# Rotary embedding on one core: tile 2 loaded whole ahead of the first store, tile 3 loaded in halves behind it, and the first store tied to a subtraction of tile 1

## The chip, the cores and the metric

The kernel runs on one core of a Trainium2 chip. The metric is the device time of one execution in microseconds, taken as the median of several executions; less is better. Beside the times there is a profile of one execution, whose time axis starts at its first instruction.

## The reference, cut to what matters

`x` has the shape (16, 512, 16, 64) in float32: batch, position, heads, 64 elements. `cos` and `sin` have the shape (512, 32), of which only the first 16 columns are used. Of each row of 64 elements the first 32 are rotated in two quarters of 16, and the last 32 pass through:

```python
rotated_first  = x1[..., :16] * cos[..., :16] - x1[..., 16:] * sin[..., :16]
rotated_second = x1[..., :16] * sin[..., :16] + x1[..., 16:] * cos[..., :16]
out = concatenate([rotated_first, rotated_second, x2], axis=-1)
```

So 33.55 MB come in and 33.55 MB go out, and each of the rotated elements costs two multiplications and one addition or subtraction.

## The kernel before, in words

The array is cut into four tiles (`T` = 4), each of 128 partitions by 16 positions (`K` = 16, called rows here) of 1,024 elements: 64 KB in each partition, 8.39 MB in a tile. A ring in SBUF holds three tiles (`NS` = 3), so that tile 3 lies where tile 0 lay, and can only be loaded when tile 0 has been stored. All loads and the stores of tiles 0, 1 and 3 are issued by SP (`load` L56, `store` L59) on one queue; the store of tile 2 and the two small loads of the tables are issued by POOL on another. SP issues in the order of the program, and an instruction that waits holds up all that is behind it on SP.

VectorE (DVE) does all the arithmetic. It first spreads the tables (L62 to L84). Then `rotate(t, lo, hi)` works rows `lo` to `hi` of tile `t` in four instructions: the product with the sine into the PSUM buffer `b_t` (L97), the product with the cosine in place (L98), a subtraction into the first quarter (L99), and an addition into the second (L106). Most calls take 8 rows, half a tile (`KC` = 8); tile 2 is worked in 8, 5 and 3 rows (`KM` = 5).

The order of the transfers is written out by hand. SP issues: load of tile 0, load of tile 1, load of the second half of tile 2; store of the first half of tile 0, store of its second half; load of the first half of tile 2, load of tile 3; store of tile 1; store of tile 3. The function `hold` ties a transfer to an instruction of DVE that it doesn't need for its data, so that it is issued no earlier than that. It is used twice: the first store of tile 0 waits for the first part of the last addition of tile 0, which is cut at row 12 for this (`KP`), and the store of tile 1 waits for the subtraction of the 5 rows of tile 2 (`near`).

Of the kernel before, what the change touches and what calls it, by code (L numbers as in the profile page):

```python
# [1 line left out]

# [4 lines left out]


@with_exitstack
def kernel(  # L10
    ctx: ExitStack,
    tc: tile.TileContext,
    x: bass.AP,
    cos: bass.AP,
    sin: bass.AP,
    out: bass.AP,
):
    nc = tc.nc
    fp32 = mybir.dt.float32
    P = 128  # L20
    B, S, H, D = x.shape
    Q = D // 4
    HF = D // 2

    K = 16
    T = B * S // (P * K)
    PB = S // K
    REP = P // PB  # L30
    R = H * D
    NS = 3
    KC = K // 2
    KM = 5
    KP = K - 4

    xf = x.rearrange("b s h d -> (b s h d)").rearrange("(t p f) -> t p f", t=T, p=P)
    of = out.rearrange("b s h d -> (b s h d)").rearrange("(t p f) -> t p f", t=T, p=P)
    cosf = cos.rearrange("(p k) j -> p (k j)", k=K)
    sinf = sin.rearrange("(p k) j -> p (k j)", k=K)  # L40

    const_pool = ctx.enter_context(tc.tile_pool(name="const", bufs=1))
    b_pool = ctx.enter_context(tc.tile_pool(name="bp", bufs=1, space=bass.MemoryType.PSUM))


    ring = const_pool.tile([P, NS, K, H, D], fp32)
    stage = const_pool.tile([P, 2, K, HF], fp32)
    spun = const_pool.tile([P, 2 * K, Q], fp32)
    packed = const_pool.tile([PB, 2 * K, Q], fp32)
    table = const_pool.tile([P, 2, K, 2, Q], fp32)  # L50

    def rows(t, lo, hi):
        return ring[:, t % NS, lo:hi].rearrange("p k h d -> p (k h d)")

    def load(t, lo=0, hi=K):
        return nc.sync.dma_start(out=rows(t, lo, hi), in_=xf[t, :, lo * R : hi * R])  # L56

    def store(t, lo=0, hi=K, queue=nc.sync):
        return queue.dma_start(out=of[t, :, lo * R : hi * R], in_=rows(t, lo, hi))  # L59


    nc.vector.memset(stage[:, :, :, 0:Q], 0.0)  # L62
    spread = stage.rearrange("(j b) t k i -> j b t (k i)", b=REP)
    nc.gpsimd.dma_start(out=spread[:, 0, 0], in_=cosf)  # L64
    nc.gpsimd.dma_start(out=spread[:, 0, 1], in_=sinf)  # L65
    load(0)
    load(1)
    load(2, KC, K)

    PQ = PB // REP
    nc.vector.stream_shuffle(  # L74
        out=spun[:],
        in_=stage.rearrange("p t k j -> p (t k) j")[:, :, 0:Q],
        mask=[j % PQ * REP for j in range(PB)],
    )
    for q in reversed(range(REP)):
        n = PQ * (q + 1)  # L80
        nc.vector.tensor_copy(out=packed[0:n], in_=spun[q * PB : q * PB + n])  # L81

    for r in range(REP):
        nc.vector.tensor_copy(  # L84
            out=table[r * PB : (r + 1) * PB].rearrange("p t k c j -> p (t k) c j"),
            in_=packed.unsqueeze(2).to_broadcast((PB, 2 * K, 2, Q)),
        )
    C = table[:, 0].rearrange("p k c j -> p k (c j)")
    Sn = table[:, 1].rearrange("p k c j -> p k (c j)")

    def rotate(t, lo, hi, cut=None):
        x1 = ring[:, t % NS, lo:hi, :, 0:HF]
        c = C[:, lo:hi].unsqueeze(2).to_broadcast((P, hi - lo, H, HF))
        s = Sn[:, lo:hi].unsqueeze(2).to_broadcast((P, hi - lo, H, HF))
        b_full = b_pool.tile([P, KC, H, HF], fp32, name="b_t")
        b_t = b_full[:, 0 : hi - lo]
        nc.vector.tensor_mul(out=b_t, in0=x1, in1=s)  # L97
        nc.vector.tensor_mul(out=x1, in0=x1, in1=c)  # L98
        first = nc.vector.tensor_sub(  # L99
            out=x1[:, :, :, 0:Q], in0=x1[:, :, :, 0:Q], in1=b_t[:, :, :, Q:HF]  # L100
        )
        ends = [hi - lo] if cut is None else [cut - lo, hi - lo]
        done = []
        for a, b in zip([0] + ends, ends):
            done.append(
                nc.vector.tensor_add(  # L106
                    out=x1[:, a:b, :, Q:HF],
                    in0=x1[:, a:b, :, Q:HF],
                    in1=b_t[:, a:b, :, 0:Q],
                )  # L110
            )
        return first, done

    def hold(transfer, point):
        tc.add_manual_dep(
            transfer.ins,
            point.ins.name,
            mybir.DependencyInfo(
                mybir.DependencyClass.Sync, mybir.DependencyReason.DATA
            ),  # L120
            reason="the store follows the loads at the DMA engines",
        )

    rotate(0, 0, KC)
    _, close = rotate(0, KC, K, cut=KP)
    hold(store(0, 0, KC), close[0])
    store(0, KC, K)
    load(2, 0, KC)
    load(3)
    rotate(1, 0, KC)  # L130
    rotate(1, KC, K)
    behind_loads = store(1)
    rotate(2, KC, K)
    near, _ = rotate(2, 0, KM)
    rotate(2, KM, KC)
    store(2, queue=nc.gpsimd)

    hold(behind_loads, near)
    rotate(3, 0, KC)
    rotate(3, KC, K)  # L140
    store(3)


# [1 line left out]
_INS = ['x', 'cos', 'sin']  # L145
_OUTS = [((16, 512, 16, 64), 'float32')]


# [23 lines left out]
```

## Time and profile before

| What | Value |
| --- | --- |
| Median of 3 runs | 161.93 us (161.56 to 161.94) |
| The profiled execution's own time | 161.67 us |
| Its span, first to last instruction | 159.8 us |
| DVE busy | 113.0 us (71%), 48 instructions |
| POOL busy | 1.9 us (1%) |
| Moved by DMA | 67.24 MB in 1504 packets |
| Load of tile 0, issue to landing | 22.2 us |
| Store of tile 1 (L59), issued at | 97.59 us |
| Store of tile 3 (L59), issued at | 131.32 us |

A span of 159.8 us lies inside a time of 161.67 us: 1.87 us are outside the first and last instruction. DMA share is the mean busy share of the 16 DMA engines; since a packet is counted where it starts and lasts up to 2.4 us, a short window can show more than 1.00, and windows that begin and end at packet borders are the ones to trust. "Issue to landing" is the time from the instruction on the queue to the arrival of the last byte; with several transfers queued it holds the wait for those ahead.

### The profile page before, as it was taken

What the parts mean: (1) busy time and instruction counts of PE and PEld (TensorE: products, weight loads), DVE (VectorE), ACT (ScalarE), POOL (GpSimd) and SP (SyncE); (2) the same over time, 40 slices, a digit from 0 to 9 for tenths busy, and PEclk for the clock granted to TensorE, in tenths of its full rate; (3) what the DMA queues carried; (4) which work ended last, traced back from release to release, by engine and by line L of the source; (5) the groups of instructions that cost most, each with busy time, mean ns of one, the idle gap of its engine ahead of it and who ended that gap; (6) DMA issues with size and microseconds to landing.
All of it is one profiled execution on the core that took longest, in us unless ns stands there. A gap on an engine that the chain in (4) does not pass through costs nothing.

```text
span 159.8 us, 120 instructions
## 1 busy us (share of the span) xinstructions
DVE 113.0 (71%) x48; POOL 1.9 (1%) x7
## 2 busy tenths in 40 slices
DVE  1000959999999999999999999999999980000000
POOL 3000000000000000000000000010000000000000
DMA  7969989899799999999999799996996996996990
GB/s 262 541 262 541 410 377 525 377 410 525 303 467 410 394 484 426 402 402 508 402 525 476 312 525 394 394 525 295 492 525 262 525 508 279 525 508 279 525 508 16
DMA packets 1504, 67.24 MB, mean 421 GB/s; under 512 B 192, under 2 KB 192, under 8 KB 224
## 3 DMA queue, kind: packets, MB, share of 16 engines
q1 hardware_dynamic: 1296, 58.72, 85.4%
q0 software_dynamic: 208, 8.52, 12.3%
HBM read 33.69 MB, written 33.55 MB: 421 GB/s over the span
## 4 chain that ended last, share of the span: by engine, by line
DVE 61%; DMA 14%; issue 5%; DVEq 1%
DVE b_t L97 22%; DVE ring L98 22%; DMA ring<-in_x_dram 14%; DVE ring L106 10%; DVE ring L99 7%; DVEq L167 1%; DVEq L97 0%
## 5 line engine op out<-in xcount | busy, mean ns | idle before, releaser
L97 DVE TENSOR_TENSOR b_t<-ring,table 128x4096 f32<-128x4096 f32 (+2 forms) x9 | 35.6, 3958 | 2.1 <-DMA ring<-in_x_dram 1.9
L98 DVE TENSOR_TENSOR ring<-ring,table 128x4096 f32<-128x4096 f32 (+2 forms) x9 | 35.6, 3950 | 0.3
L99 DVE TENSOR_TENSOR ring<-ring,b_t 128x2048 f32<-128x2048 f32 (+2 forms) x9 | 18.4, 2050 | 0.3
L106 DVE TENSOR_TENSOR ring<-ring,b_t 128x2048 f32<-128x2048 f32 (+3 forms) x10 | 18.4, 1853 | 0.0
L74 DVE LOAD_MASK_SELECT spun<-stage x1 | 0.0, 14 | 14.4 <-DMA stage<-in_sin_dram 14.4
L84 DVE COPY table<-packed 32x1024 f32<-32x1024 f32 x4 | 2.7, 684 | 0.1
L59 POOL DMA_DIRECT2D out_dram<-ring x1 | 0.6, 562 | 101.8 <-DVE ring L106 101.8
L81 DVE COPY packed<-spun 32x512 f32<-32x512 f32 (+3 forms) x4 | 1.7, 416 | 0.1
L62 DVE MEMSET stage<- 128x512 f32 x1 | 0.5, 485 | 0.9 <-PEq L156 0.9
L74 DVE STREAM_SHUFFLE spun<-stage 128x512 f32<-128x512 f32 x1 | 0.7, 721 | 0.0
L64 POOL DMA_DIRECT2D stage<-in_cos_dram x1 | 0.6, 644 | 1.3 <-DVE stage L62 1.3
L65 POOL DMA_DIRECT2D stage<-in_sin_dram x1 | 0.5, 535 | 0.0
L156 POOL MEMSET const-bfloat16-1.0<- 128x1 bf16 x1 | 0.1, 102 | 0.0
L156 POOL MEMSET const-float32-0.0<- 128x1 f32 x1 | 0.1, 99 | 0.2 <-issue 0.2
L156 POOL MEMSET const-float32-1.0<- 128x1 f32 x1 | 0.1, 99 | 0.0
L156 POOL MEMSET const-uint8-127<- 128x1 uint8 x1 | 0.1, 99 | 0.0
## 6 DMA issues: line engine op xcount, KB each, us to landing
ring<-in_x_dram SPq DMA_DIRECT2D x2, 4096.0 KB, 40.8
out_dram<-ring SPq DMA_DIRECT2D x2, 4096.0 KB, 17.4
stage<-in_cos_dram POOLq DMA_DIRECT2D x1, 64.0 KB, 9.0
stage<-in_sin_dram POOLq DMA_DIRECT2D x1, 64.0 KB, 13.4
ring<-in_x_dram SPq DMA_DIRECT2D x3, 28.9
out_dram<-ring SPq DMA_DIRECT2D x2, 31.1
out_dram<-ring POOLq DMA_DIRECT2D x1, 39.6
```

The lines of the kernel that those rows point to most:

```text
L59: return queue.dma_start(out=of[t, :, lo * R : hi * R], in_=rows(t, lo, hi))
L62: nc.vector.memset(stage[:, :, :, 0:Q], 0.0)
L64: nc.gpsimd.dma_start(out=spread[:, 0, 0], in_=cosf)
L65: nc.gpsimd.dma_start(out=spread[:, 0, 1], in_=sinf)
L74: nc.vector.stream_shuffle(out=spun[:], in_=stage.rearrange("p t k j -> p (t k) j")[:, :, 0:Q], mask=[j % PQ * REP for j in range(PB)],)
L81: nc.vector.tensor_copy(out=packed[0:n], in_=spun[q * PB : q * PB + n])
L84: nc.vector.tensor_copy(out=table[r * PB : (r + 1) * PB].rearrange("p t k c j -> p (t k) c j"), in_=packed.unsqueeze(2).to_broadcast((PB, ...
L97: nc.vector.tensor_mul(out=b_t, in0=x1, in1=s)
L98: nc.vector.tensor_mul(out=x1, in0=x1, in1=c)
L99: first = nc.vector.tensor_sub(out=x1[:, :, :, 0:Q], in0=x1[:, :, :, 0:Q], in1=b_t[:, :, :, Q:HF])
L106: nc.vector.tensor_add(out=x1[:, a:b, :, Q:HF], in0=x1[:, a:b, :, Q:HF], in1=b_t[:, a:b, :, 0:Q],)
L167: with _tile.TileContext(nc) as tc:
```

## The change

Tile 2 is loaded whole as the third load. Tile 3 is loaded in two halves, one issued behind the landing of each half of the store of tile 0. The two stores of tile 0 are written behind both rotations of tile 0, and the first of them is held by the subtraction of the first 5 rows of tile 1. Tile 1 is worked in 5, 5 and 6 rows where it was worked in 8 and 8. The cut addition of tile 0 becomes one instruction again. Tile 2 is worked in 8, 5 and 3 rows as before, but from its first row on. The store of tile 1 is tied to another instruction of the 5 rows there: to the product with the cosine (L97 after, L98 before), and no longer to the subtraction (L98 after, L99 before) that follows it.

```diff
     load(0)
     load(1)
-    load(2, KC, K)
+    load(2)
...
     rotate(0, 0, KC)
-    _, close = rotate(0, KC, K, cut=KP)
-    hold(store(0, 0, KC), close[0])
-    store(0, KC, K)
-    load(2, 0, KC)
-    load(3)
-    rotate(1, 0, KC)
-    rotate(1, KC, K)
+    rotate(0, KC, K)
+    halves = [(0, KC), (KC, K)]
+    behind_loads = [store(0, lo, hi) for lo, hi in halves][0]
+    for lo, hi in halves:
+        load(3, lo, hi)
+    _, near = rotate(1, 0, KM)
+    hold(behind_loads, near)
+    rotate(1, KM, 2 * KM)
+    rotate(1, 2 * KM, K)
     behind_loads = store(1)
-    rotate(2, KC, K)
-    near, _ = rotate(2, 0, KM)
-    rotate(2, KM, KC)
+    rotate(2, 0, KC)
+    near, _ = rotate(2, KC, KC + KM)
+    hold(behind_loads, near)
+    rotate(2, KC + KM, K)
     store(2, queue=nc.gpsimd)
 
-    hold(behind_loads, near)
     rotate(3, 0, KC)
     rotate(3, KC, K)
     store(3)
```

`rotate` loses its argument `cut` and returns two other instructions: the product with the cosine (`scaled`) and the subtraction (`first`). So `near` stands for two things. For tile 1 it is the second value returned, the subtraction; for tile 2 it is the first, the product. The lines of the changed file that say so:

```python
        scaled = nc.vector.tensor_mul(out=x1, in0=x1, in1=c)
...
        return scaled, first
```

More of the change, by code (lines that the diff above doesn't have):

```diff
@@ L34 @@
     KM = 5
-    KP = K - 4
     xf = x.rearrange("b s h d -> (b s h d)").rearrange("(t p f) -> t p f", t=T, p=P)
@@ L89, with rotate @@
     Sn = table[:, 1].rearrange("p k c j -> p k (c j)")
-    def rotate(t, lo, hi, cut=None):
+    def rotate(t, lo, hi):
         x1 = ring[:, t % NS, lo:hi, :, 0:HF]
@@ L97, in rotate @@
         nc.vector.tensor_mul(out=b_t, in0=x1, in1=s)
-        nc.vector.tensor_mul(out=x1, in0=x1, in1=c)
+        scaled = nc.vector.tensor_mul(out=x1, in0=x1, in1=c)
         first = nc.vector.tensor_sub(
@@ L101, in rotate @@
         )
[L102 to L112, printed above, removed]
+        nc.vector.tensor_add(
+            out=x1[:, :, :, Q:HF], in0=x1[:, :, :, Q:HF], in1=b_t[:, :, :, 0:Q]
+        )
+        return scaled, first
     def hold(transfer, point):
```

## The prediction

> **What bounds the kernel now.** I read the page's DMA parts first, then the chain of work that ended last, then the busy time by window cut at the stages, and last the timeline around the instructions that release stores.
>
> ```profile
> DVE 61%; DMA 14%; issue 5%; DVEq 1%
> ...
> q1 hardware_dynamic: 1296, 58.72, 85.4%
> q0 software_dynamic: 208, 8.52, 12.3%
> HBM read 33.69 MB, written 33.55 MB: 421 GB/s over the span
> ```
>
> The chain names DVE for 61% of the span, and on that alone the kernel looks bound by arithmetic. The two queues speak against it: their packets fill 85.4 + 12.3 = 97.7% of all 16 DMA engines' span. The chain follows semaphores, and a store that was released by DVE but then stands behind other bytes is told as DVE's. So the question is whether DMA ever stood still. The windows, cut at the borders of the stages (columns: window, length, DVE busy, POOL busy, clock, DMA share, GB/s):
>
> ```profile
> 1.70:51.00 49.30, 32.86 (x20) 1.18 (x2) 1.00 1.00 428
> 51.10:70.60 19.50, 19.36 (x6) 0.00 (x0) 1.00 1.00 430
> 70.60:99.80 29.20, 28.92 (x12) 0.00 (x0) 1.00 1.00 431
> 99.80:158.50 58.70, 31.22 (x12) 0.56 (x1) 1.00 0.99 429
> ```
>
> The first row is loads alone, the second the stores of tile 0 alone, the third loads again, the fourth the last three stores. The share is 0.99 to 1.00 in each, and reading and writing run at the same 428 to 431 GB/s. From 1.70 to 158.50 us the DMA engines do nothing but move the bytes that must be moved. The time is therefore 1.70 us ahead of the first byte, 156.80 us of full DMA, 1.30 us to the end of the span at 159.8, and 1.87 us outside it: 161.67 us. DVE ends its last instruction at 131.3 us and is 27 us early.
>
> The changeover from loads to the store of tile 1 shows no hole either (borders at packet ends; same columns):
>
> ```profile
> 97.39:99.80 2.41, 2.38 (x3) 0.00 (x0) 1.00 1.01 435
> 99.80:102.22 2.42, 2.39 (x2) 0.00 (x0) 1.00 1.00 433
> 102.22:104.64 2.42, 2.35 (x4) 0.00 (x0) 1.00 1.00 433
> ```
>
> **The change part by part.** The bytes are the same. SP still issues nine transfers: four of half tiles and five of whole ones become again four and five (a half load of tile 2 twice and half stores twice, against half stores twice and half loads of tile 3 twice). So DMA's own work is the same 156.80 us, and the change costs or saves only where it opens or closes a hole. I therefore time DVE first, and then lay each issue of SP against what is still queued.
>
> The rows that price DVE (start, duration, engine, line, operation; the row of SPq merges the issues of the last two stores on SP, and starts with that of tile 1):
>
> ```profile
> 36.51 4.43 DVE L97 TENSOR_TENSOR b_t<-ring,table 128x4096 f32<-128x4096 f32 x1
> ...
> 50.02 4.43 DVE L97 TENSOR_TENSOR b_t<-ring,table 128x4096 f32<-128x4096 f32 x1
> ...
> 90.35 2.83 DVE L97 TENSOR_TENSOR b_t<-ring,table 128x2560 f32<-128x2560 f32 x1
> 93.22 2.83 DVE L98 TENSOR_TENSOR ring<-ring,table 128x2560 f32<-128x2560 f32 x1
> 96.08 1.49 DVE L99 TENSOR_TENSOR ring<-ring,b_t 128x1280 f32<-128x1280 f32 x1
> ...
> 97.59 34.08 SPq L59 DMA_DIRECT2D out_dram<-ring  x2
> 99.00 1.77 DVE L97 TENSOR_TENSOR b_t<-ring,table 128x1536 f32<-128x1536 f32 x1
> ...
> 104.44 4.43 DVE L97 TENSOR_TENSOR b_t<-ring,table 128x4096 f32<-128x4096 f32 x1
> ```
>
> Five rows take 99.00 - 90.35 = 8.65 us, three take 104.44 - 99.00 = 5.44, eight take 13.44 (36.51 less the 23.07 at which the first call starts). Six lie on the line between five and eight: 8.65 + 4.79 / 3 = 10.25.
>
> The cut addition goes: the second half of tile 0 took 50.02 - 36.51 = 13.51 and takes 13.44, so tile 1 starts at 49.95. Tile 1 in 5, 5 and 6 rows costs 8.65 + 8.65 + 10.25 = 27.55 against 2 x 13.44 = 26.88; tile 2 starts at 77.50, against 76.91 before: **DVE is 0.59 us later from there to its end**, since tiles 2 and 3 keep their sizes. Tile 2's whole load lands at about 61.7 us (below), 16 us ahead of its use, so DVE doesn't wait.
>
> *First store.* It waits for the subtraction of tile 1's first five rows, which ends 97.57 - 90.35 = 7.22 us into such a call: 49.95 + 7.22 = 57.17 us (48.88 before). Behind it on SP stand the second store of tile 0 and both loads of tile 3, the latter needing this store's landing anyway. The loads ahead now end half a tile later: load 1 landed at 42.3 us (issued 1.17, 41.1 to landing) and load 0 at 23.0, so a tile takes 19.3 and load 2 lands at 61.7. The store is queued 4.5 us before that; before the change it was 52.15 - 48.88 = 3.3. No hole; were the cover gone, each us of lateness would be a us of the end.
>
> *Loads of tile 3.* Half a tile takes 9.7 to 9.9 us (the two half stores landed at 61.9 and 71.8). The first half store lands at 61.7 + 9.9 = 71.6, the seventh half tile, as the second half store was before. SP issues the first half load then, with the second half store, 9.7 us of bytes, still running. That lands at about 81.5, and the second half load is issued with the first, again 9.7 us, in front of it. Loads end at about 100.8, as before (71.91 + 28.9). DVE wants these halves at 105.0 and 118.5. Cost: nothing, hidden by the half transfer in front each time.
>
> *Store of tile 1.* Here the diff does more than its words say. In tile 2 `near` is now the first value returned, the product with the cosine, and no longer the subtraction. The product ends 93.22 + 2.83 - 90.35 = 5.70 us into the call: 77.50 + 13.44 + 5.70 = 96.64, so the issue comes at 96.66, 0.93 us earlier than the 97.59 before in spite of DVE's delay. The lead over the end of loads grows from 3.2 to 4.1 us. Cost: nothing, for the profile shows no hole with the shorter lead.
>
> *Stores of tiles 2 and 3.* POOL's store is issued at 104.71 + 0.59 = 105.3, with nearly all of tile 1's 19 us queued in front. SP's last store is issued at 131.32 + 0.59 = 131.91. It took 27.5 us from issue to landing (the list of DMA issues, cut at that instant), against 19.3 for a tile alone: 8.2 us of other bytes were in front, 7.6 stay. Cost: nothing.
>
> *Could there be a price that the trace doesn't show?* Stores are now issued with leads of 4.5 and 4.1 us. Generating their descriptors beside running transfers could slow these; the rows around the first release (49.88:51.09, share 1.03 for 1.21 us) allow 0.04 us each. From below, the most that any order could win is the time in which DMA runs under its best rate: 67.24 MB at 433 GB/s is 155.3, so 156.80 holds 1.5 us, of which the first 3.1 us (window 1.70:4.80 at 338 GB/s) hold 3.1 x (1 - 338/433) = 0.7, which the change doesn't touch. The bounds are -0.8 and +0.1; I take 0, which the 0.99 to 1.00 of the shares lies nearest to.
>
> The sum: 161.67 + 0 = 161.67 for the profiled execution. That lies 0.26 below the median of the runs shown (161.93), so I forecast **161.9** for a median.
>
> Weighed against the Trainium skill, "DMA: Bandwidth & Descriptors": its section "Where 436 GB/s comes from" lets HBM's share of a core, about 358 GB/s, bind transfers between HBM and SBUF; by that the 67.24 MB would need 188 us. This trace shows 428 to 431 in every stage, so the measurement decides. The section "Anatomy of one DMA" gives each transfer a fixed cost of about 2.0 us, which speaks against cutting the load of tile 3 in two where it would be exposed; nine such costs unhidden would be 18 us, and the trace has room for at most 1.5 in all.
>
> **The rivals.**
> 1. *DVE's end governs after all*, slower. The chain runs through DVE to 131.3 and then through the last store; were 27.5 us a fixed cost behind its issue, the 0.59 us of DVE would reach the end: 161.67 + 0.59 = 162.26, 162.5 on the median. For it: the chain. Against it: 8.2 us of the 27.5 are queue. It decides only from the point where DVE is over 8.2 us later, unless queue 1's first packet has to wait that long for a turn beside queue 0.
> 2. *A better packed DMA*, faster. Leads are longer, and what is under the best rate outside the start comes back: 161.67 - 0.8 = 160.9, or 161.1 on the median. Against it: no window shows the loss in one place.
> 3. *The hold doesn't do what it says.* The first store could be issued as soon as tile 0 is done, at 50.0; it would still stand behind load 2 on its queue, and the time would be 161.9 again.
>
> **How the numbers follow.** My forecast and rival 3 together have 0.76, rival 1 0.13, rival 2 0.11. A difference of 0.3% (0.49 us) is about what a measurement of this kernel tells from no change: the three runs spread by 0.38. Rival 1 with its 0.59 is over that, rival 2 with 0.8 too, so the chances are 0.11 faster, 0.76 the same, 0.13 slower. The range takes in rival 1's 162.5 with 0.1 for the descriptors, to 162.6, and most of the way to rival 2, to 161.2.
>
> **What would show it.** The DMA share stays 0.99 to 1.00 in all four stages, whose borders move to about 61, 81 and 100 us. The first store is issued near 57.2, the first half load of tile 3 near 71.9, the second near 81.7, the store of tile 1 near 96.7 and released by the product with the cosine, the last store near 131.9 and landing near 158.8, with some 27 us to landing. I am wrong if a window at one of these changeovers falls clearly below 1.00, if packets run slower in one stage, or if the last store lands 0.5 us or more away from 158.8.

## The result, and the profile after

The changed kernel takes 162.62 us (median of 6 runs, 162.45 to 162.87) against 161.75 us for the kernel before in the same comparison (161.51 to 161.94): a ratio of 1.006, 95% interval 1.0048 to 1.0073. It is about 0.9 us slower, where no difference was forecast. The profiled execution took 162.87 us with a span of 160.9 us; that of the kernel before took 161.67 us, so the two traces differ by 1.2 us. Of these, 1.1 us lie inside the span (160.92 against 159.85) and 0.1 outside it: time less span is 1.95 us after and 1.82 before, and their other executions on record agree with that to within the 0.1 us to which their spans are noted.

The DMA parts of the changed kernel's page (queue: packets, MB, share of 16 engines' span):

```profile
q1 hardware_dynamic: 1296, 58.72, 85.5%
q0 software_dynamic: 208, 8.52, 12.2%
HBM read 33.69 MB, written 33.55 MB: 418 GB/s over the span
```

Packets and bytes are those of before, and the shares make 97.7% of the span in all, as before. There is no hole, and yet the same bytes take 1.1 us more of the span. So packets must be slower somewhere, and the busy share cannot tell: a packet that is held up counts as busy. The rate can. The busy time by window of the changed kernel, cut where the first packet of each stage begins (window, length, DVE busy, POOL busy, clock, DMA share, GB/s):

```profile
1.70:58.30 56.60, 40.03 (x22) 1.17 (x2) 1.00 1.00 430
58.30:61.72 3.42, 3.35 (x3) 0.00 (x0) 1.00 1.00 287
61.72:71.40 9.68, 9.58 (x5) 0.00 (x0) 1.00 1.00 433
71.40:81.08 9.68, 9.61 (x4) 0.00 (x0) 1.00 1.00 433
81.08:100.44 19.36, 19.15 (x9) 0.00 (x0) 1.00 1.01 433
100.44:159.50 59.06, 31.23 (x12) 0.56 (x1) 1.00 0.98 426
```

The second row is the loss: from 58.30 to 61.72 us the last packets of the load of tile 2 run at 287 GB/s with the share at 1.00. (It holds 15 of the last 16 packets, one for each DMA engine; the sixteenth starts just ahead of the window.) The other rows run at 426 to 433 GB/s, where the stages of the kernel before had 428 to 431. The same row of the kernel before, the last packets of its loads in front of the store of tile 0, is at full rate:

```profile
49.88:51.09 1.21, 1.18 (x2) 0.00 (x0) 1.00 1.03 433
```

So are its last packets in front of the store of tile 1, 435 GB/s from 97.39 to 99.80. What happened 1 us ahead of the slow row stands in SP's timeline of the changed kernel (start, duration, issue; two issues are merged in a row):

```profile
57.26 0.83 SPq L58 DMA_DIRECT2D out_dram<-ring  x2
72.75 10.14 SPq L55 DMA_DIRECT2D ring<-in_x_dram  x2
96.72 35.60 SPq L58 DMA_DIRECT2D out_dram<-ring  x2
```

The two stores of tile 0 were issued from 57.26 us on (48.88 before). The list of DMA issues, cut at the third load, gives its time to landing:

```profile
ring<-in_x_dram SPq DMA_DIRECT2D x1, 61.3
```

Issued at 1.64 us, load 2 lands at 63.0, which is 20.6 us behind load 1 (42.4), where load 1 was 19.35 behind load 0: 1.25 us too late. From there on nothing more is lost. The landings of the two traces follow. The order of the transfers differs, so the table counts half tiles moved: the seventh is the second half store of tile 0 before and the first one after, the eighth the load of tile 2's first half before and the second half store after.

| Landing of | before, us | after, us | later by |
| --- | --- | --- | --- |
| load 1 | 42.3 | 42.4 | 0.1 |
| seventh half tile moved | 71.8 | 72.7 | 0.9 |
| eighth | 81.4 | 82.5 | 1.1 |
| last load | 100.8 | 101.9 | 1.1 |
| last store | 158.8 | 159.9 | 1.1 |

### The profile page after: what moved, and what is told of

The parts are those of the page before. It is cut to its first block, busy times and chain, and to the rows that moved or that the text cites. A ratio compares the mean times of both kernels' runs of the same rounds, so it can differ in the third digit from the quotient of the medians.

```text
span 160.9 us, 120 instructions
## 1 busy us (share of the span) xinstructions
DVE 113.4 (70%) x51; POOL 1.9 (1%) x7
## 4 chain that ended last, share of the span: by engine, by line
DVE 62%; DMA 14%; issue 5%; DVEq 1%
DVE b_t L96 22%; DVE ring L97 22%; DMA ring<-in_x_dram 14%; DVE ring L101 10%; DVE ring L98 7%; DVEq L161 1%; DVEq L96 0%
## 5 line engine op out<-in xcount | busy, mean ns | idle before, releaser
L96 DVE TENSOR_TENSOR b_t<-ring,table 128x4096 f32<-128x4096 f32 (+3 forms) x10 | 35.8, 3580 | 2.2 <-DMA ring<-in_x_dram 1.9
L97 DVE TENSOR_TENSOR ring<-ring,table 128x4096 f32<-128x4096 f32 (+3 forms) x10 | 35.7, 3571 | 0.3
L98 DVE TENSOR_TENSOR ring<-ring,b_t 128x2048 f32<-128x2048 f32 (+3 forms) x10 | 18.6, 1860 | 0.3
L101 DVE TENSOR_TENSOR ring<-ring,b_t 128x2048 f32<-128x2048 f32 (+3 forms) x10 | 18.5, 1853 | 0.0
## 6 DMA issues: line engine op xcount, KB each, us to landing
ring<-in_x_dram SPq DMA_DIRECT2D x2, 4096.0 KB, 19.3
```

Source lines behind the costliest of these rows:

```text
L97: scaled = nc.vector.tensor_mul(out=x1, in0=x1, in1=c)
L98: first = nc.vector.tensor_sub(out=x1[:, :, :, 0:Q], in0=x1[:, :, :, 0:Q], in1=b_t[:, :, :, Q:HF])
L101: nc.vector.tensor_add(out=x1[:, :, :, Q:HF], in0=x1[:, :, :, Q:HF], in1=b_t[:, :, :, 0:Q])
```

## The experiments

In what follows the lead is the time by which a store is issued ahead of the landing of the load in front of it, had that load run at its own rate: 4.5 us in the changed kernel at the first store, 3.1 to 3.3 us in the kernel before. (The expectations on record count it to the last packets instead, some 0.7 to 1.1 us less.) The first theory, LEAD, says that a store queued early behind a load slows the last packets of that load. Its rivals were the packet sizes and the two stores issued together.

**1. The first store one instruction later** (addition of tile 1's first five rows).

```diff
-    _, near = rotate(1, 0, KM)
+    _, _, near = rotate(1, 0, KM)      # rotate returns its addition as well
```

> The changed kernel with one edit: the first store waits for the addition of tile 1's first five rows (ends at 58.6 us) and no longer for the subtraction (57.2). Theory LEAD (a store whose descriptors reach the engines before these begin the last load packet slows that packet, which began at 58.3 to 58.9 in the changed kernel): the store now comes too late to do it; load 2 lands 60.1 us after its issue where it was 61.3, and the time is about 161.6. Theory SIZES (packets of 64 KB followed by packets of 32 KB cost the last one, whenever the store is issued): 61.3 and 162.6, unchanged. Theory TWO (two stores queued together behind a load are too many): 61.3 and 162.6, unchanged.

Load 2 landed 60.4 us after its issue, most of the way from 61.3 to LEAD's 60.1, but the median was 163.61 us (ratio 1.0101, 1.0059 to 1.0144) where LEAD said 161.6. The profiled execution took 162.36 us, the other three 163.6 to 163.8. So LEAD has the place right, its time is wrong, and the time is lost again elsewhere.

**2. Tile 2 in half transfers, all ahead of the first store.**

```diff
-    load(2)
+    load(2, 0, KC)
+    load(2, KC, K)
```

> The changed kernel with tile 2 loaded as two half transfers ahead of the first store, so that the last load packets are of 32 KB like those of the store. LEAD: the store is issued as early as before (57.2), so the last packets are still slowed, though each is half as long; load 2's second half lands between 60.3 and 61.3 us after its issue, time 161.9 to 162.6. SIZES: no packet is slowed, 60.1 and 161.6. TWO: 61.3 and 162.6.

162.55 us (1.007, 1.0048 to 1.0091); the second half landed at 62.8 us, where load 1's 42.2 and 19.35 make 61.6. The packets' size is not it.

**3. The second store of tile 0 much later.**

```diff
+    later, _ = rotate(1, KM, 2 * KM)
+    hold(second, later)                # second: the store of rows 8 to 15
```

> The changed kernel with the second store of tile 0 held as well, by the product with the cosine of tile 1's second five rows (ends at 64.4 us); the first store stays as it is. LEAD and SIZES: unchanged, load 2 lands after 61.3 us and the time is 162.6. TWO: 60.1 and 161.6.

162.63 us (1.0056, 1.0033 to 1.0079), load 2 landed at 62.7 us. One queued store is enough.

**4. The kernel before, its store of tile 1 issued 1.4 us earlier.** `rotate` returns its product with the cosine, and the hold takes it.

```diff
-    near, _ = rotate(2, 0, KM)
+    _, _, near = rotate(2, 0, KM)      # the product, not the subtraction
```

> The kernel before with one edit: the store of tile 1 waits for the product with the cosine of tile 2's five rows (96.05 us) where it waited for the subtraction (97.57); its last load packets are of 64 KB and its stores too, and one store is issued alone. LEAD: the last load packets began at 97.4 to 97.9, over 1 us behind the new issue, so they are slowed by up to 1.3 us; load 3 lands about 1 us later than 28.9 us after its issue, and the time is 162.3 to 163. SIZES and TWO: unchanged, 28.9 and 161.75.

162.66 us (1.0054, 1.0036 to 1.0072). The window over the last packets of load 3 in this run:

```profile
97.20:100.10 2.90, 2.87 (x3) 0.00 (x0) 1.00 1.09 362
```

and the list of DMA issues, cut at load 3:

```profile
ring<-in_x_dram SPq DMA_DIRECT2D x1, 30.0
```

Load 3 needs 30.0 us from issue to landing where it needed 28.9, and the last packets run at 362 GB/s where they ran at 435. An edit of nothing but the store's lead, in the other kernel and at the other changeover, costs what the change costs.

**5 and 6. Does the loss grow with the lead?** In the changed kernel the first store without a hold, and with the hold one and a half us earlier.

```diff
-    _, near = rotate(1, 0, KM)
-    hold(behind_loads, near)
+    rotate(1, 0, KM)                   # run 5; run 6: near, _ = rotate(1, 0, KM)
```

> The changed kernel without a hold on the first store: its two halves are issued as soon as tile 0's halves are worked, near 36.6 and 50.0 us, 24 and 11 us ahead of the end of the loads. ONCE (a store that is queued early behind a load slows it by about 1.2 us in all, however early): load 2 lands 61.3 us after its issue, time 162.6. RATE (the load is slowed by about a third for as long as a store stands behind it): load 2 lands after 64 us or more, time over 165. WINDOW (the cost falls only on a lead of some 3 to 4 us, since the leads of 4.2 at the store of tile 1 cost 0.1 to 0.2): 60.1 us, time 161.7.

> The changed kernel with the first store held by the product with the cosine of tile 1's first five rows (ends near 55.7 us), 1.5 us earlier than the subtraction; its lead over the end of the loads is about 5 us. ONCE: load 2 lands after 61.3 us, time 162.6. RATE: after 61.8, time 163.1. WINDOW: after 60.1 to 60.4, time 161.7.

162.64 us (1.0068, 1.0053 to 1.0083) and 162.65 us (1.0072, 1.0057 to 1.0087). The window over the last load packets in run 5, whose first store was issued at 36.38 us:

```profile
58.28:61.65 3.37, 3.30 (x3) 0.00 (x0) 1.00 1.02 311
```

The slow stretch begins at the same packets and lasts as long, with a lead of 25 us. ONCE holds; a loss that grows, and one that falls on leads of 3 to 4 us alone, are out.

**7, 8 and 11. Both holds late, and the second hold alone.** Run 7 takes run 1 and gives the store of tile 1 back its subtraction; run 11 is the same again; run 8 gives it back in the changed kernel alone.

```diff
-    near, _, _ = rotate(2, KC, KC + KM)
+    _, near, _ = rotate(2, KC, KC + KM)
```

> The changed kernel with both holds late: the first store on the addition of tile 1's five rows (58.6, lead about 2.4 us), the store of tile 1 on the subtraction of tile 2's five rows (98.2, as the kernel before names it), where the changed kernel has the product with the cosine. ONCE, RATE and WINDOW alike: both leads are down to those of the kernel before, load 2 lands after 60.1 to 60.4 us, load 3's second half 19.1 to 19.3 after its issue, time 161.7. If the 163.6 of the first experiment is not the store of tile 1's doing, it stays near 163.6.

> The changed kernel with the store of tile 1 held by the subtraction (98.2 us) as in the kernel before, and the first store as in the changed kernel. If the first store alone makes the change slower (ONCE, RATE, WINDOW alike): load 2 lands after 61.3 us, time 162.5, some 0.15 below the changed kernel at most. If the store of tile 1 bears most of it: 161.9.

> The kernel with both holds late once more, for a second trace. If its 163.07 us come from one or two engines that fall behind where stores give way to loads, load 2 lands 60.1 us after its issue again, tile 3's second half near 102 us again, and the time is 162.9 to 163.3. If the engine that fell behind was chance, the time is 161.7.

Run 8 gave 162.64 us (1.0061, 1.0044 to 1.0078): the hold that my prediction made much of is worth nothing here. Runs 7 and 11 gave 163.07 us (1.0096, 1.008 to 1.0111) and 162.60 us (1.0067, 1.0045 to 1.0089): all three theories failed on the time. Yet the loss at the first changeover is gone, as the window over the last packets of load 2 in run 7 shows, and after it load 2's time to landing:

```profile
58.33:60.79 2.46, 2.42 (x2) 0.00 (x0) 1.00 0.95 400
```

```profile
ring<-in_x_dram SPq DMA_DIRECT2D x1, 60.1
```

(The window again holds 15 of the 16 packets: 400 GB/s over 2.46 us is what 15 packets make at full rate, and the same 15 in 3.42 us made the 287 of the changed kernel.) What was won is lost behind it. The list of DMA issues of run 7, cut at the second half load of tile 3:

```profile
ring<-in_x_dram SPq DMA_DIRECT2D x1, 4096.0 KB, 20.4
```

In the changed kernel that transfer took 19.3 us. Run 11's trace is neither of the two that were expected of it: load 2 lands 60.3 us after its issue, but that transfer takes 19.5 us and the last load lands at 101.3.

**9, 12 and 15. What else the order of loads could do**, each in the kernel before: the load of tile 2's first half issued 13 us later (run 9), tile 3 in halves (run 12), and one of these halves ahead of tile 2's (run 15).

```diff
-    load(2, 0, KC)                     # run 9
+    queued = load(2, 0, KC)
+    hold(queued, half[0])              # behind rotate(1, 0, KC); half[0]: its addition
...
-    load(3)                            # run 12; run 15 has load(3, 0, KC) ahead of load(2, 0, KC)
+    load(3, 0, KC)
+    load(3, KC, K)
```

> The kernel before with one edit: the load of the first half of tile 2, issued at 50.4 us right behind the stores of tile 0, waits for the first addition of tile 1 (ends near 63.4 us), and so is issued while the stores run, as the loads of tile 3 are in the changed kernel. LATE LOAD (a load issued only during the stores makes some engines lose time where stores give way to loads, as at 79 to 81 us in the run with both holds late): it lands later than the 81.4 us of the kernel before by 0.3 us or more, time 162.2 to 163. Otherwise: lands at 81.4, time 161.5.

> The kernel before with tile 3 loaded in two halves, each behind the landing of one half store of tile 0, and everything else as it was. ONCE and LATE LOAD: the first half load is issued near 62 and the second near 72, both behind the load of tile 2's first half, so nothing changes: landing near 100.8, time 161.5. If half loads of tile 3 are what costs: 162 or more.

> The kernel before with tile 3 in halves and the first of them issued ahead of the first half of tile 2, so that a half of tile 3 follows the stores as in the changed kernel. ORDER: it lands later than 81.4 us by 0.4 us or more, time 162.3 or more. PACKETS and ROWS: it lands near 81.4; DVE then waits some 0.7 us for the half of tile 2 (lands near 91.1, wanted at 90.35), which the queue in front of the last store hides, time 161.6 to 162.0.

Run 9: 161.55 us (1.0002, 0.9991 to 1.0014), nothing. Run 12: 161.96 us (1.0026, 1.0013 to 1.0039). Run 15: 161.99 us (1.0034, 1.0021 to 1.0048), the half of tile 3 behind the stores landing at 81.2 us. A load issued late doesn't matter. Halves of tile 3 cost 0.4 to 0.6 us by the times, but hardly anything inside the span: in the two traces the last loads land at 100.6 and 100.7 us and the last store at 158.5 and 158.6, no later than before, and the spans of all executions have medians of 159.75 and 159.8 us against 159.7 and 159.6 for the kernel before. What grows is the time outside the span, from 1.8 to about 2.2 us in every execution of both runs. What it is spent on isn't shown; it doesn't follow the number of transfers alone, for runs 2 and 13, which have a half transfer more than the changed kernel, spend 1.7 us there where that kernel spends 1.95.

**10. The part that failed, alone in the kernel before**: its first store one instruction earlier.

```diff
-    _, close = rotate(0, KC, K, cut=KP)
-    hold(store(0, 0, KC), close[0])
+    close, _ = rotate(0, KC, K, cut=KP)
+    hold(store(0, 0, KC), close)
```

> The kernel before with one edit: the first store waits for the last subtraction of tile 0 (ends at 47.7 us) and not for the first part of the addition (48.86), so that its lead over the end of the loads is about 3.6 us where it was 2.4. ONCE: the load of tile 2's second half lands about 1 us later than 50.5 us after its issue, and the time is 162.4 to 162.7. If the lead matters only in the changed order of loads: 50.5 and 161.5.

162.53 us (1.0062, 1.004 to 1.0085). With everything of the change left out but the lead (47.62 us in place of 48.88), the kernel before becomes as slow as the changed one. The window over its last two rounds of load packets, 32 of 32 KB, which take twice 1.21 us at full rate:

```profile
48.64:51.99 3.35, 3.32 (x3) 0.00 (x0) 1.00 1.00 313
```

**13 and 14. What is left with both holds late**: tile 2 in halves as in run 2 (run 13), and tile 1 in 8 and 8 rows with the first store on the product of the first 8 (run 14).

```diff
-    _, _, near = rotate(1, 0, KM)
+    near, _, _ = rotate(1, 0, KC)      # run 14, then rotate(1, KC, K)
```

> The kernel with both holds late (162.6 and 163.07 us) with tile 2 loaded as two half transfers, so that the last load packets ahead of the first store are of 32 KB, as in the kernel before. PACKETS (what is left of the loss with late holds comes from 64-KB load packets in front of 32-KB store packets): load 3's first half lands near 91.1, time 161.6. ORDER (it comes from a half of tile 3 following the stores, whatever the packets) and ROWS (it comes from tile 1 in 5, 5 and 6 rows): unchanged, 162.6 to 163.1.

> The kernel with both holds late, with tile 1 worked in 8 and 8 rows again; the first store waits for the product with the cosine of the first 8 (ends near 58.9 us, where the addition of 5 rows ended at 58.6). ROWS: 161.6. PACKETS and ORDER: unchanged, 162.6 to 163.1.

162.38 us (1.0046, 1.0022 to 1.007) and 163.62 us (1.0133, 1.0115 to 1.0151). Neither the packets nor the rows of tile 1 bear the rest. Run 14 issued its last store at 131.26 us, earlier than the changed kernel by 0.7, and was, with run 1, the slowest of all.

**16, 17 and 18. The lead from the other side, and the two stores apart.** Run 16 holds the first store of the kernel before by the whole cut addition; run 18 also holds the second store, by the first product of tile 1; run 17 holds the second store in run 7.

```diff
-    hold(store(0, 0, KC), close[0])
+    hold(store(0, 0, KC), close[1])    # runs 16 and 18
+    hold(second, later)                # runs 17 and 18
```

> The kernel before with the first store waiting for the whole of the cut addition (50.0 us) and no longer for its first part (48.86): a lead of 1.3 us. ONCE: there is little left to win, since the kernel before loses some 0.1 us there; time 161.4 to 161.6, unless descriptors need longer than 1.3 us, and then a hole of up to 1 us opens: 161.8 to 162.5.

> The kernel with both holds late, with the second store of tile 0 held as well, by the product with the cosine of tile 1's second five rows (ends near 64.4 us), so that the two stores are no longer issued 0.4 us apart. APART (in all runs with a late first store that lost time where stores give way to loads, the two stores were issued back to back; in the kernel before they were 1.1 us apart): tile 3's first half lands near 91.1, its second near 100.8, time 161.6. POINT (it is the lead alone: a first store late enough to cost nothing at its own changeover makes the next one cost): unchanged, second half near 101.3 to 102, time 162.4 to 163.1.

> The kernel before with its first store at 50.0 us (as in the run before with 162.25 us) and the second held until the product with the sine of tile 1's first rows (ends near 54.5 us). APART: the loss where stores give way to loads goes, load 3 lands 100.7, time 161.5. POINT: load 3 lands 101.1 as with the stores together, time 162.2.

Run 16: 162.25 us (1.0052, 1.0033 to 1.007), without a hole at the first changeover and without the 161.4 to 161.6 that ONCE expected. Run 17: 161.91 us (1.0038, 1.0013 to 1.0063); five of its seven runs took 161.6 to 161.9, the others 162.5 and 163.2. Run 18: 162.13 us (1.0033, 1.002 to 1.0045). The second half load of tile 3 in run 17's list of DMA issues:

```profile
ring<-in_x_dram SPq DMA_DIRECT2D x1, 4096.0 KB, 19.1
```

So taking the stores apart goes with the return of the lost time in the changed order (20.4 us in run 7, 19.5 in its repeat, run 11, and 19.1 here), and not in the order of the kernel before, where load 3 lands at 101.1 us in run 18 as in run 16. APART and POINT each explain one of the two.

The traces that lost time, in one table worked out from the issue and landing times. "First" is how much longer than its own 19.35 us (a half: 9.68) the last load ahead of the stores took behind load 1. "Later" is how much longer than in the trace of the kernel before (28.9 us from the second store of tile 0 to the end of the loads), or of the changed one (19.3), the rest of the loads took. Between the two stretches lie the half stores of tile 0, which are in neither column: from the landing of the load to that of the second store it is 19.5 to 19.9 us in all traces, the longest in runs 7 and 11.

| Run | First store issued, us | First, us | Later, us | Profiled execution, us |
| --- | --- | --- | --- | --- |
| before | 48.88 | 0.2 | 0 | 161.67 |
| after | 57.26 | 1.3 | 0 | 162.87 |
| 1 | 58.42 | 0.5 | 0.4 | 162.36 |
| 2, 3, 5, 6, 8 | 57.10, 57.20, 36.38, 55.62, 57.41 | 1.2, 1.0, 1.3, 1.2, 1.2 | 0.1 or less | 162.55 to 162.84 |
| 7 and 11 | 58.61, 58.63 | 0.0, 0.3 | 1.1, 0.2 | 162.96, 162.32 |
| 13 and 14 | 58.56, 58.87 | 0.1, 0.2 | 1.1, 1.9 | 162.62, 163.74 |
| 17 | 58.38 | 0.3 | -0.2 | 161.57 |
| 4 | 49.02 | 0.0 | 1.2 | 162.72 |
| 10 | 47.62 | 1.0 | -0.1 | 162.20 |
| 16 and 18 | 49.87, 49.82 | 0.0, 0.0 | 0.4, 0.5 | 161.94, 161.87 |

From the last load's landing to the last store's it is 57.9 to 58.0 us in all of them: what a kernel loses inside its span, it loses ahead of that. No run beats the kernel before.

The packets themselves narrow the place further. At full rate a packet of 64 KB takes 2.42 us and one of 32 KB takes 1.21. In all 20 traces together 351 packets on SP's queue between 6 and 104 us take over 0.2 us longer, and 344 of them belong to the last two rounds ahead of a change between loads and stores (a round is one packet on each of the 16 engines) or start within half a round of it; the other seven follow closely behind one. In the changed kernel they are the 16 last packets of load 2 (3.3 to 4.0 us each) and five, far less late, ahead of the store of tile 1. In run 7 they are mostly last packets of the stores of tile 0, at 79 us, and two of the 16 engines are held up most (one packet there took 2.19 us). In run 16 they are the last packets of those stores at 69.2 us (up to 2.12) and the last ones of load 3 at 97.5 (up to 3.08). So a loss that has gone from one change of direction can turn up at the next.

## Why the prediction was wrong, point by point

**Right: what bounds the kernel.** The bytes set the time; DVE does not. Run 14, with DVE 0.7 us earlier at the end, is slower than the changed kernel, and run 17, with the changed kernel's DVE work, is 1.3 us faster in its trace. So rival 1, which had the sign, is refuted as a mechanism: DVE came 0.65 us later, 0.59 worked out (last store issued at 131.97, forecast 131.91), and the last store's 27.9 us to landing still hold over 8 us of queue.

**Right: the schedule.** The first store at 57.26 us (forecast: at the end of the subtraction, 57.17), the store of tile 1 at 96.72 (96.66), in the list of waits behind the product with the cosine:

```profile
SPq L58 <- DVE ring L97: 13.7, 1, 13.7
```

**Right inside the span: the halves of tile 3 and the third load whole cost nothing at their places**; the changed kernel runs at 433 GB/s from 61.72 to 100.44. The sum had taken the 1.87 us outside the span as fixed. They are not: 0.13 us more in the changed kernel, 0.4 us more in runs 12 and 15. The 2.0 us for each transfer, which the prediction weighed against this, stand in the Trainium skill's section "Anatomy of one DMA" for transfers issued by POOL; in the stretch at 433 GB/s four transfers of SP follow each other without a gap of that kind.

**Wrong, and the step that failed: "First store ... The store is queued 4.5 us before that ... No hole."** There was no hole, and I took that for no cost. I treated more lead as more cover, which can only help. The runs show that it has a price: at the first changeover, a store that stands behind a load from 4.2 us or more ahead of its landing makes the load's last packets slower, by 1.0 to 1.3 us in all, whether the lead is 4 or 25 us (runs 2, 3, 5, 6, 8, 10), in one store or two (run 3), with packets of 32 or 64 KB (run 2). With leads of 2.7 to 3.2 us it is 0.0 to 0.5, with 2.0 nothing. At the other changeover the same step costs as much in the kernel before (run 4), but not in the changed one. Two of the signs that the prediction had named came true: packets ran slower in one stage, and the last store landed at 159.9 us, 1.1 away from 158.8. The third, a share below 1.00, did not; the busy share was the wrong thing to watch.

**Wrong: the bound on an unseen price.** The step "Could there be a price that the trace doesn't show?" took its upper end, 0.1 us, from the row around the first release of the kernel before. But that row shows the very lead that costs little. No row of the trace had a store queued early behind a load, so the row bounded nothing, and the range, which ended at 162.6, missed the median by 0.02 us. That it came so near is luck: its upper end was rival 1's 162.5 with 0.1 added, and rival 1's mechanism played no part. Rival 3 stumbled on the same: it put a first store issued as soon as tile 0 is done at no cost, and run 5, whose two stores were issued so, at 36.4 and 49.8 us, took 162.64.

**Wrong: the store of tile 1.** I gave its earlier issue no cost. In the changed kernel that holds (run 8), and in the kernel before the same step costs the full price (run 4). The lead was about 5.1 us in the one (101.9 - 96.7) and 4.4 us in the other (28.9 us behind 71.7, less 96.2), and run 10, with 4.0 us there, lost nothing in its trace. So the lead alone doesn't decide: 4.4 us cost the full price in one kernel, 5.1 us cost nothing in the other, and that difference is open.

**What stays open.** When the first store is late enough to pay nothing, the next changeovers often pay instead (runs 7, 13, 14, 16, 18), and the kernel before sits between, at 0.2 and 0. I have shown where, but not why. Late loads, packet sizes, the rows of tile 1 and a half of tile 3 behind the stores were tried, each in one of the two orders, and are not it, and the stores' distance explains run 17 but not run 18. That run 1's other executions lost 1.2 us more than its trace is open too. The trace gives the place of the slow packets and not what holds them up. The Trainium skill, "DMA: Bandwidth & Descriptors", section "Two DMAs through the same engine are not ordered", says that the descriptors (the orders that tell a DMA engine what to move) of one queue of an engine start in order but overlap, with reading and writing in separate queues; a store could then begin to read SBUF while the load ahead is still writing it. No run here shows that this is what happens. The same page's section "Rules for kernel authors" advises issuing a DMA early to hide its fixed cost. For these stores the measurement differs: run 10 issues one 1.26 us earlier and is 1 us slower.

## What to carry to other kernels

Where DMA is busy all the time, read the rate at each changeover and not only the busy share: a share of 1.00 at 287 GB/s is lost time that no hole shows. A store issued early behind a running load was not free here; when a kernel holds its stores to a chosen instruction, treat that lead as tuned: one instruction earlier (run 10) or later (run 16) cost as much as the whole change of order. Look also at what lies outside the span before a few tenths of a microsecond are put down to a transfer. And a row bounds an unseen cost only if the condition in question occurs in it.

## What the runs showed of the hardware that was not expected

- The price of a store queued early behind a load is paid once, at the first changeover: 1.0 to 1.3 us with leads from 4 to 25 us, in the last packets of the load (311 GB/s over 3.4 us in run 5, in place of 433). At the store of tile 1 in the changed kernel a lead of 5.1 us cost nothing.
- A store late enough to avoid it (58.6 in place of 57.3 us) left its mark later: at 79 us, in the last packets of the stores, and in tile 3's second half load, which took 20.4 us to land in place of 19.3 (run 7; 19.5 in its repeat).
- The time outside the first and last instruction differs from program to program: 1.8 us in the kernel before, 1.95 in the changed one, 2.2 in runs 12 and 15, 1.7 in runs 2 and 13.
- Reading and writing HBM run at one rate here: 433 GB/s for stores alone (61.72 to 81.08 us) and for loads alone (81.08 to 100.44).
